# Attention slots of a hybrid encoder layer: VectorE's order of two minima, two normalisations and a gated product

## The chip, the core and the metric

The kernel runs on one core of a Trainium2 chip. Its time is the device time of one execution in microseconds (us), as the median of several runs. A profile of one execution gives, for every engine, the start and duration of each instruction. The engines are TensorE (PE, with its weight loads as PEld), VectorE (DVE), ScalarE (ACT), GpSimd (POOL) and SyncE (SP). Each works through its own instructions in the order in which the program issues them, and they wait for one another through semaphores.

## The reference, cut to what matters

One layer of an encoder on 2048 tokens of width 1024: an adaptive RMSNorm, one input projection, a group of eight neighbourhood-attention heads (head width 64) on a grid of 32 rows by 64 columns, a group of four bidirectional mLSTM heads, an output projection, a residual sum and a last RMSNorm. The change touches the attention:

```python
s = jnp.einsum('bhrcd,bhrjkd->bhrcjk', qg, kg).astype(jnp.float32) + bias[None]
s = jnp.where(col_mask[:, None, :], s, -jnp.inf)
p = jax.nn.softmax(s.reshape(B, NA_HEADS, rows, GRID_W, kh * GRID_W), axis=-1).reshape(s.shape)
o = jnp.einsum('bhrcjk,bhrjkd->bhrcd', p, vg)
...
na_out = neighbourhood_attention(na_q, na_k, na_v, rpb) * jax.nn.silu(na_z)
```

Every query sees a window of 8 rows by 16 columns of keys. The scores get a learned bias, go through a softmax, weigh the values, and the result is multiplied by a gate.

## The kernel before, in words

The input projection and the mLSTM fill the first 1011 us or so of the trace. Then comes the attention stage (`phase2`), in which the output projection runs as filling between the pieces of attention.

**Tiles.** The grid is cut into 16 patches of 8 rows by 16 columns, 128 queries each. A patch sees 11 to 15 rows by 24 or 32 columns of keys, so 264, 288, 352, 360, 384 or 480 scores per query. A *unit* is one patch and one pair of heads (two heads, numbered j = 0 and 1); there are 64 units. A *slot* works on two new units and finishes the two old ones of the slot before: `slot(m)` for m = 0 to 32, of which the last has no new units. The order of all instructions in the stage is the order of the calls (`manual_schedule`); nothing is reordered.

**What a slot issues, by engine, before the change:**

- TensorE: twelve score products into pS (L1341, four buffers, one per unit and head); the old units' value products into pO (L1384, one buffer); six products of the filling (`pump`, L1429: output projection; L866, the last of the input projection, in the first slots); the transposes of the first unit's head 0 (L1369) into pT, which has **one buffer**; five of filling; the transposes of head 1; five; those of the second unit's head 0; four; head 1; four. Slots 0 to 2 have 8, 7, 7, 7, 7 of filling instead.
- VectorE: for each unit and head in turn one pass (L1349) that adds a bias table to the scores, with their sign turned, writes the result into one of four buffers pbuf and returns the row minimum (four *minima* in a slot); then the *normalisation* of the first unit, a reciprocal of its two sums (L1359) and two scalings of pbuf (L1361); then the *gated product* of the old units (L1391), which reads pO; then the normalisation of the second unit.
- ScalarE: behind each minimum the exponential (L1350), in place, with the sum of the row read out from an accumulator; later, behind each group of transposes, the copy of pT into SBUF (L1371). Between them come, where the filling asks for them, squares of finished output rows (L1436; the calls of `finish`), the split of the mixed features into high and low parts (L1399 on ScalarE, L1404 on VectorE), and in the first slots DMA issues and splits of weights.
- SyncE: where the bias table that a minimum has just read isn't needed any more, the load of the table that takes its place (`load_tab`, L1313), issued behind that minimum and used in the next slot; and the queries for two slots later (`load_q`, L1256). GpSimd loads values (L1269), gates (L1279) and rows of x.

In the last filling of a slot VectorE often still adds a finished piece of the output projection to x (L1434), whose square ScalarE issues in the next slot, behind that slot's four exponentials and ahead of its first copy.

**Where it stands in the code.** `scores` (L1327) issues the score products of both units, then minimum, exponential and table load for each unit and head. `normalised` (L1356) issues a unit's reciprocal and scalings, `turned` (L1364) its transposes and copies, `values` (L1374) the value products, `gated` (L1387) the gated product. `slot` (L1545) calls them.

Of the kernel before, what the change touches and what calls it, by code (L numbers as in the profile page):

```python
# [62 lines left out]
class Kernel:  # L63
# [1142 lines left out]
    def phase2(self):  # L1206
# [45 lines left out]
        def load_q(i):  # L1252
            if 2 * i >= NU:
                return
            b, c0 = units[2 * i][0], min(units[2 * i][1], units[2 * i + 1][1])
            (nc.gpsimd, nc.gpsimd, nc.scalar, nc.sync)[min(i, 3)].dma_start(qs[i % 3].bitcast(F32), self.d_qna[:, c0 // 2, b].rearrange("e p c q -> p e c q"))  # L1256
# [53 lines left out]
        def load_tab(u, j):  # L1310
            b, ct = units[u]
            nk = geo[b][4]
            (nc.gpsimd if u < 2 else nc.sync).dma_start(tabs[place[u]][j][:, :nk], self.d_t[PR_T[b // 4]][PC_T[b % 4]][2 * ct + j])  # L1313
# [10 lines left out]
        split, done = set(), []  # L1324
        U = {}

        def scores(pair):  # L1327
            made = {}
            for u in pair:
                b, ct = units[u]  # L1330
                pr, pc, nr, nkc, nk, rpc, nch = geo[b]
                q, c = qs[(u // 2) % 3], ct % 2
                rs = slice(PR_R0[pr], PR_R0[pr] + nr)
                cs = slice(PC_C0[pc], PC_C0[pc] + nkc)
                keys = [kk[ct][:, e * T : (e + 1) * T].rearrange("p (r c) -> p r c", c=GRID_W)[:, rs, cs] for e in range(2)]
                made[u] = [pS.tile([P, 512], F32, tag="pS", name=f"pS_{u}_{j}")[:, :nk] for j in range(2)]
                for n, (e, f) in enumerate(((0, 0), (1, 0), (0, 1))):
                    for j, ps in enumerate(made[u]):
                        js = slice(j * HD, (j + 1) * HD)
                        o = ps.rearrange("p (r c) -> p r c", c=nkc)  # L1340
                        nc.tensor.matmul(o, q[js, e, c, :], keys[f][js], start=(n == 0), stop=(n == 2))  # L1341
            for u in pair:
                nk = geo[units[u][0]][4]
                pts = []
                sums = few.tile([P, 2], F32, tag="sums", bufs=3, name=f"sums_{u}")
                for j, ps in enumerate(made[u]):
                    pt = pbuf[(2 * u + j) % 4]
                    mn = few.tile([P, 1], F32, tag="mn", bufs=4, name=f"mn_{u}_{j}")
                    nc.vector.tensor_tensor_reduce(pt[:, :nk], ps, tabs[place[u]][j][:, :nk], 1.0, 3e38, ALU.add, ALU.min, mn)  # L1349
                    nc.scalar.activation(pt[:, :nk], pt[:, :nk], AF.Exp, bias=mn, scale=-1.0, accum_out=sums[:, j : j + 1])  # L1350
                    pts.append(pt)
                    if u in follows:
                        load_tab(follows[u], j)
                U[u] = (pts, sums)

        def normalised(u):  # L1356
            nk = geo[units[u][0]][4]
            pts, sums = U[u]
            nc.vector.reciprocal(sums, sums)  # L1359
            for j in range(2):  # L1360
                nc.vector.tensor_scalar(pts[j][:, :nk], pts[j][:, :nk], sums[:, j : j + 1], None, ALU.mult)  # L1361
            U[u] = pts

        def turned(u, j):  # L1364
            pr, pc, nr, nkc, nk, rpc, nch = geo[units[u][0]]
            cs = rpc * nkc
            ps = pT.tile([P, 4, P], F32, tag="pT", name=f"pT_{u}_{j}")
            for i in range(nch):
                nc.tensor.transpose(ps[:cs, i, :], U[u][j][:, i * cs : (i + 1) * cs], self.ident)  # L1369
            t = p.tile([P, 4, P], F32, tag="pt", bufs=4, name=f"pt_{u}_{j}")  # L1370
            nc.scalar.activation(t[:cs, :nch, :], ps[:cs, :nch, :], AF.Copy)  # L1371
            U[u][j] = t

        def values(pair):  # L1374
            po = pO.tile([P, 2, P], F32, tag="pO", name=f"pO_{pair[0]}")
            for u in pair:
                b, ct = units[u]
                nch = geo[b][6]
                pt = U.pop(u)
                for i in range(nch):  # L1380
                    v, n = L[b]["v"][i]
                    for j in range(2):
                        h = 2 * ct + j
                        nc.tensor.matmul(po[j * HD : (j + 1) * HD, ct % 2, :], v[:n, h * HD : (h + 1) * HD], pt[j][:n, i, :], start=(i == 0), stop=(i == nch - 1))  # L1384
            return po

        def gated(pair, po):  # L1387
            b, ct = units[pair[0]]
            c0 = ct // 2 * 2
            z = zs[pos[b] % 2][:, c0 : c0 + 2, :]  # L1390
            nc.vector.tensor_mul(z, po, z)  # L1391
# [120 lines left out]
        def loads(n):  # L1512
            b, ct = units[n]
            i = n % 4
            nb = after.get(b)
            if b == last_b and i == 1:
                load_x(b)
            if nb is not None and i:
                load_v(nb, 1 if i < 3 else 4)
                if i == 2 and b != b0:  # L1520
                    load_z(nb)
# [8 lines left out]
        def step():  # L1530
            if self.between:
                self.between.pop(0)()
            self.step_todo()

        def finish():
            while self.squares:
                self.squares.pop(0)()

        def mixed(b, half):
            mix_high(b, half)  # L1540
            mix_low(b, half)
            if half:
                self.queue.append(outproj(b))

        def slot(m):  # L1545
            new = (2 * m, 2 * m + 1) if 2 * m < NU else ()
            old = (2 * m - 2, 2 * m - 1) if m else ()
            if m:
                load_q(m + 2)
            if new:  # L1550
                scores(new)
            if old:
                po = values(old)
            if new:
                normalised(new[0])
            if old:
                gated(old, po)
            if new:
                normalised(new[1])
            b = units[old[0]][0] if m > 2 and old[0] % 4 == 2 else None  # L1560
            if not new:
                mixed(b, 1)
                mixed(b, 0)
                for _ in range(2):
                    self.pump(12)
                    finish()
                    step()
                return
            fills = [8, 7, 7, 7, 7] if m < 3 else [6, 5, 5, 4, 4]
            for n in range(-1, 4):  # L1570
                if n >= 0:
                    turned(new[n // 2], n % 2)
                    if n % 2:
                        step()
                    finish()
                    if n in (1, 2) and b is not None:
                        mixed(b, n % 2)
                    if n in (0, 2):
                        loads(new[n // 2])
                    if n == 1 and self.reloads:  # L1580
                        self.reloads.pop(0)()
                for fn in extra.pop((m, n), ()):
                    fn()
                self.pump(fills[n + 1])
            if m == 2:
                self.pump(max(0, self.left) + 1)
                self.owed = 0
                mixed(b0, 1)
                mixed(b0, 0)

        with self.tc.manual_schedule():
            for m in range(NU // 2 + 1):
                slot(m)
            while len(done) < len(patches):
                finish()
                while self.between:
                    self.between.pop(0)()
                while self.todo:
                    self.todo.pop(0)()
                self.pump(24)  # L1600
            for fn in self.between + self.todo:
                fn()
# [77 lines left out]
```

## Time and profile before

| what | value |
|---|---|
| runs | 1382.79, 1383.26 and 1388.96 us; median 1383.26 |
| profiled execution | 1385.16 us |
| its span, first to last instruction | 1383.4 us |
| mean granted clock of TensorE | 0.989 |
| slots of the attention stage | 32 with new units, beginning at 1015.2 to 1344.9 us of the span |
| length of a slot | 9.4 to 12.8 us |

The span is the time from the first to the last instruction of the profiled execution; 1.8 us of the execution lie around it. In a row of a timeline stand the start in us from the span's beginning, the duration, the engine, the line, the operation and its operands (out<-in), and in square brackets how long the engine had been idle before it and what released it. Rows of groups give the busy time in us, the mean in ns, and the idle time ahead with its releasers. Consecutive instructions of one engine overlap in such rows by about a tenth of a microsecond, since they are pipelined.

### The profile page before, as it was taken

What the parts mean: (1) busy time and instruction counts of PE and PEld (TensorE: products, weight loads), DVE (VectorE), ACT (ScalarE), POOL (GpSimd) and SP (SyncE); (2) the same over time, 40 slices, a digit from 0 to 9 for tenths busy, and PEclk for the clock granted to TensorE, in tenths of its full rate; (3) what the DMA queues carried; (4) which work ended last, traced back from release to release, by engine and by line L of the source; (5) the groups of instructions that cost most, each with busy time, mean ns of one, the idle gap of its engine ahead of it and who ended that gap; (6) DMA issues with size and microseconds to landing.
All of it is one profiled execution on the core that took longest, in us unless ns stands there. A gap on an engine that the chain in (4) does not pass through costs nothing.

```text
span 1383.4 us, 23357 instructions
## 1 busy us (share of the span) xinstructions
PE 1291.3 (93%) x8204; PEld 1104.9 (80%) x8204; DVE 792.3 (57%) x2428; ACT 531.8 (38%) x1123; POOL 284.1 (21%) x306
## 2 busy tenths in 40 slices
PE   2989998998999999999989999899998999999996
PEld 2889998998887778788878878778876777778775
DVE  6683324111355569246767866767736666667664
ACT  4642334423232233213313322323346555555552
POOL 4343212424101011001212101212201211112121
PEclk9999999999999999999999999999999999999998
DMA  9799449787557685554675788555588996867871
GB/s 321 223 290 228 122 97 238 175 204 189 149 110 210 151 191 160 164 157 144 184 219 182 229 237 284 165 159 159 176 249 251 209 228 171 187 184 183 205 182 47
DMA packets 243272, 263.29 MB, mean 190 GB/s; under 512 B 31814, under 2 KB 200006, under 8 KB 243154
## 3 DMA queue, kind: packets, MB, share of 16 engines
q1 hardware_dynamic: 151774, 186.18, 49.8%
q0 software_dynamic: 20496, 36.21, 10.8%
q10 hardware_dynamic: 70884, 39.40, 9.9%
q8 instruction: 65, 1.06, 0.3%
q14 instruction: 53, 0.43, 0.1%
HBM read 177.18 MB, written 92.72 MB: 195 GB/s over the span
## 4 chain that ended last, share of the span: by engine, by line
PE 46%; DMA 11%; issue 4%; DVE 4%; POOL 1%; ACT 1%; ACTq 0%; SPq 0%; DVEq 0%; POOLq 0%
PE pq L866 19%; PE y L1429 9%; DMA tab<-d_t 4%; PE pT L1369 3%; PE pO L1384 2%; PE pS L1341 2%; PE pi L1090 2%; DMA kv<-d_ck 2%; PE px L1088 2%; PE pc L429 2%; PE pc L430 2%; PE pc L431 2%; DMA d_mix<-zt 2%; PE dc L1036 1%; DMA d_qna<-qst 1%
## 5 line engine op out<-in xcount | busy, mean ns | idle before, releaser
L866 PE MATMUL pq<-hhi,whi_a 128*128 128x512 f32 x512 | 208.6, 407 | 1.2 <-ACT u L773 0.8
L866 PE MATMUL pq<-hlo,whi_a 128*128 128x512 f32 x512 | 208.9, 408 | 0.0
L866 PE MATMUL pq<-hhi,wlo_a 128*128 128x512 f32 x512 | 208.2, 407 | 0.0
L866 PEld LDWEIGHTS pq<-hhi,whi_a 128*128 128x128 f32 x512 | 97.3, 190 | 18.9 <-ACT u L773 1.2
L866 PEld LDWEIGHTS pq<-hlo,whi_a 128*128 128x128 f32 x512 | 97.2, 190 | 16.8 <-issue 0.5
L866 PEld LDWEIGHTS pq<-hhi,wlo_a 128*128 128x128 f32 x512 | 97.3, 190 | 16.6
L1371 ACT ACTIVATE pt<-pT 96x384 f32<-96x384 f32 (+3 forms) x128 | 65.8, 514 | 84.5 <-PE pT L1369 81.3
L1350 ACT ACTIVATE pbuf<-pbuf,mn 128x480 f32<-128x480 f32 (+5 forms) x128 | 76.1, 595 | 54.1 <-DVE mn L1349 53.8
L1429 PE MATMUL y<-hhi,whi_a 128*128 128x512 f32 x256 | 90.6, 415 | 0.5 <-ACT whi_a L1399 0.5
L1429 PE MATMUL y<-hhi,wlo_a 128*128 128x512 f32 (+1 forms) x272 | 90.6, 399 | 0.2 <-ACT y L1436 0.2
L1349 DVE CUSTOM_DVE_ANT_0 pbuf<-pS,tab 128x480 f32<-128x480 f32 (+5 forms) x128 | 63.3, 540 | 40.3 <-PE pS L1341 29.6
L840 POOL TENSOR_TENSOR wlo_a<-rawq,whi_a 128x1024 fp32r<-128x1024 f32 x20 | 48.6, 2430 | 169.8 <-ACT whi_a L839 144.9
L1112 POOL TENSOR_TENSOR hm<-hm,ck 128x128 f32<-128x128 f32 x64 | 26.4, 413 | 260.3 <-DVE hm L1111 183.4
L429 PE MATMUL pvo<-whi_b,hhi 128*128 128x256 f32 x256 | 74.1, 289 | 5.7 <-DVE stvo L499 5.7
L1093 ACT ACTIVATE num<-px,gtile 128x129 f32<-128x129 f32 x120 | 38.3, 366 | 105.7 <-PE px L1088 88.0
L1020 DVE TENSOR_SCALAR wv<-kv,gtile 128x129 f32<-128x129 f32 x120 | 38.4, 329 | 67.1 <-DMA kv<-d_ck 33.5
L1369 PE MATMUL pT<-ident,pbuf 128*128 128x128 f32 (+2 forms) x416 | 66.8, 273 | 10.0 <-DVE pbuf L1361 8.5
L1369 PEld LDWEIGHTS pT<-ident,pbuf 128*128 128x128 f32 (+2 forms) x416 | 50.3, 136 | 31.9 <-issue 11.6
L430 PE MATMUL pvo<-wlo_b,hhi 128*128 128x256 f32 x256 | 72.8, 285 | 0.0
L431 PE MATMUL pvo<-whi_b,hlo 128*128 128x256 f32 x256 | 72.8, 284 | 0.0
L714 ACT ACTIVATE dec<-dec,gtile 128x128 f32<-128x128 f32 x128 | 42.0, 392 | 71.4 <-POOL dec L710 68.3
L499 DVE TENSOR_TENSOR stvo<-pvo,brow 128x256 f32<-128x256 f32 x64 | 26.5, 419 | 68.6 <-PE pvo L431 56.4
(295 smaller groups left out, 3432.6 us busy)
## 6 DMA issues: line engine op xcount, KB each, us to landing
ck<-d_ck SPq DMA_DIRECT2D x64, 384.5 KB
kv<-d_ck SPq DMA_DIRECT2D x120, 128.5 KB
rawq<-in_w_main_dram SPq DMA_DIRECT2D x28, 512.0 KB
raw<-in_w_main_dram SPq DMA_DIRECT2D x20, 512.0 KB
d_ck<-stvo SPq DMA_DIRECT2D x16, 514.0 KB
x<-in_x_dram SPq DMA_DIRECT2D x16, 512.0 KB
wada<-in_w_ada_dram SPq DMA_DIRECT2D x32, 256.0 KB
dec<-d_mneg SPq DMA_DIRECT2D x32, 256.0 KB
```

What stands on the lines that cost most here:

```text
L429: nc.tensor.matmul(ps, lhi(k), rhi(k), start=(k == 0), stop=False)
L430: nc.tensor.matmul(ps, lhi(k), rlo(k), start=False, stop=False)
L431: nc.tensor.matmul(ps, llo(k), rhi(k), start=False, stop=(k == KT - 1))
L714: nc.scalar.activation(t[:, d, o, :], t[:, d, o, :], AF.Exp, bias=self.cols["g"][:, d, h, c : c + 1])
L840: nc.gpsimd.tensor_tensor(lo[:, :, cs], raw, hi[:, :, cs].bitcast(F32), ALU.subtract)
L866: nc.tensor.matmul(patch_ps(ps) if patch else ps, w, self.htok(h, g, k, patch), start=(k == 0 and n == 0), stop=(k == KT - 1 and n == 2))
L1020: nc.vector.tensor_scalar(wv, tiles[d, i][:, 128:257], self.cols["w"][:, d, h, c : c + 1], None, ALU.mult)
L1349: nc.vector.tensor_tensor_reduce(pt[:, :nk], ps, tabs[place[u]][j][:, :nk], 1.0, 3e38, ALU.add, ALU.min, mn)
L1350: nc.scalar.activation(pt[:, :nk], pt[:, :nk], AF.Exp, bias=mn, scale=-1.0, accum_out=sums[:, j : j + 1])
L1369: nc.tensor.transpose(ps[:cs, i, :], U[u][j][:, i * cs : (i + 1) * cs], self.ident)
L1371: nc.scalar.activation(t[:cs, :nch, :], ps[:cs, :nch, :], AF.Copy)
L1429: nc.tensor.matmul(y, m[:, k, :], w[k][:, cs], start=(k == 4 and n == 0), stop=(k == 3 and n == 2))
```

## The change

`scores` is cut in two. `products` issues the score products of both units, `scored` the minima, the exponentials and the table loads. Between the first unit's and the second unit's minima `scored` now calls `normalised` for the first unit. The gated product follows when `scored` is done, so behind the second unit's minima; the second unit's normalisation stays last. On TensorE, ScalarE, SyncE and GpSimd the order of instructions stays the same; on VectorE it becomes: two minima, normalisation of the first unit, two minima, gated product, normalisation of the second unit.

```diff
-        def scores(pair):
+        def products(pair):
             made = {}
             for u in pair:
...
                         nc.tensor.matmul(o, q[js, e, c, :], keys[f][js], start=(n == 0), stop=(n == 2))
+            return made
+
+        def scored(pair, made):
             for u in pair:
                 nk = geo[units[u][0]][4]
...
                 U[u] = (pts, sums)
+                if u == pair[0]:
+                    normalised(u)
...
             if new:
-                scores(new)
+                scored(new, products(new))
             if old:
-                po = values(old)
-            if new:
-                normalised(new[0])
-            if old:
-                gated(old, po)
+                gated(old, values(old))
             if new:
                 normalised(new[1])
```

## The prediction

> **What bounds the kernel now.** I began with the page: its first table says which engine has no room.
>
> ```profile
> PE 1291.3 (93%) x8204; PEld 1104.9 (80%) x8204; DVE 792.3 (57%) x2428; ACT 531.8 (38%) x1123; POOL 284.1 (21%) x306
> ```
>
> TensorE works 93% of the span and VectorE 57%, so a VectorE order can matter only where TensorE waits for it. The change touches the attention stage alone (1011 to 1355 us of the trace), so next comes the table of waits of TensorE and VectorE in that window (engine and line, released by: total us, times, longest):
>
> ```profile
> PE pT L1369 <- DVE pbuf L1361: 8.5, 6, 2.2
> PE pT L1369 <- ACT pt L1371: 1.6, 1, 1.6
> ...
> DVE pbuf L1349 <- DMA tab<-d_t: 9.8, 11, 2.5
> ```
>
> Six times in 32 slots a slot's first transposes wait for the normalisation, 8.5 us in all. That is the most that the change can win. Everywhere else TensorE runs through, and the question is whether it still will.
>
> Third I read the timeline of one slot engine by engine: slot 29, an ordinary one of 360 scores (start, duration, engine, line). VectorE:
>
> ```profile
> 1326.77 0.53 DVE L1349 CUSTOM_DVE_ANT_0 pbuf<-pS,tab 128x360 f32<-128x360 f32 x1
> ...
> 1328.64 0.17 DVE L1359 RECIPROCAL sums<-sums 128x2 f32<-128x2 f32 x1
> 1328.84 0.73 DVE L1361 TENSOR_SCALAR pbuf<-pbuf,sums 128x360 f32<-128x360 f32 x2
> 1329.48 0.42 DVE L1391 TENSOR_TENSOR zs<-pO,zs 128x256 f32<-128x256 f32 x1
> ```
>
> ScalarE and TensorE in the same slot:
>
> ```profile
> 1327.93 0.58 ACT L1350 ACTIVATE pbuf<-pbuf,mn 128x360 f32<-128x360 f32 x1
> 1328.42 0.18 ACT L1350 ACTIVATION_READ_ACCUMULATOR pbuf<-pbuf,mn 128x1 f32 x1
> 1328.51 0.58 ACT L1350 ACTIVATE pbuf<-pbuf,mn 128x360 f32<-128x360 f32 x1
> ...
> 1329.09 0.58 ACT L1350 ACTIVATE pbuf<-pbuf,mn 128x360 f32<-128x360 f32 x1
> ...
> 1329.67 0.58 ACT L1436 ACTIVATE y<-xr 128x512 f32<-128x512 f32 x1
> ...
> 1330.28 0.47 ACT L1371 ACTIVATE pt<-pT 120x384 f32<-120x384 f32 x1
> ```
> ```profile
> 1329.53 0.49 PE L1369 MATMUL pT<-ident,pbuf 128*120 128x128 f32 x3
> ...
> 1331.03 0.49 PE L1369 MATMUL pT<-ident,pbuf 128*120 128x128 f32 x3
> ```
>
> See the coupling. pT has one buffer. The second transposes (1331.03) may start only when the copy of the first (L1371) has left pT, and on ScalarE that copy stands behind all four exponentials and, here, a square (L1436). It ends at 1330.28 + 0.47 = 1330.75, 0.28 us before TensorE arrives. So the exponentials of the second unit lie on TensorE's path already, with almost nothing to spare.
>
> **What the change moves.** No instruction is added or removed. On VectorE the minima of the second unit go behind the first unit's reciprocal and its two scalings. The reciprocal needs both exponentials of the first unit, so VectorE now stands still for them with the second minima queued behind. Today that wait is covered: by the time four minima are done the exponentials are too (reciprocal 1328.64, accumulator read out by 1328.42 + 0.18 = 1328.60). Slot 0 shows the naked hand-overs:
>
> ```profile
> 1018.41 0.19 ACT L1350 ACTIVATION_READ_ACCUMULATOR pbuf<-pbuf,mn 128x1 f32 x1
> ...
> 1021.41 0.49 ACT L1371 ACTIVATE pt<-pT 96x384 f32<-96x384 f32 x1 [2.81 <-DMA v<-d_vna]
> ```
> ```profile
> 1018.63 0.17 DVE L1359 RECIPROCAL sums<-sums 128x2 f32<-128x2 f32 x1 [0.19 <-ACT pbuf L1350]
> ```
> ```profile
> 1021.95 0.53 PE L1369 MATMUL pT<-ident,pbuf 128*96 128x128 f32 x3 [1.57 <-ACT pt L1371]
> ```
>
> ScalarE to VectorE: 1018.63 - 1018.60 = 0.03. Copy's end to transposes: 1021.95 - 1021.90 = 0.05.
>
> *Shift of the second exponentials, slot 29.* Readout ends 1328.60; + 0.03 reciprocal; + 0.20 to the scalings (1328.64 to 1328.84); + 0.73 for both; - 0.09, by which the next instruction overlaps them (1329.48 against 1329.57); + 0.53 minimum; + 0.04 to its exponential: 1330.04 instead of 1328.51, a shift of **1.53 us**. In general it is 0.27 + pair of scalings + one minimum. Other widths come from VectorE's groups by form (busy, mean ns of one):
>
> ```profile
> L1349 DVE CUSTOM_DVE_ANT_0 pbuf<-pS,tab 128x480 f32<-128x480 f32 x32 | 19.4, 653 | 9.6 <-PE pS L1341 9.0 <-DMA tab<-d_t 0.6
> ...
> L1361 DVE TENSOR_SCALAR pbuf<-pbuf,sums 128x480 f32<-128x480 f32 x32 | 14.0, 479 | 0.6
> ...
> L1349 DVE CUSTOM_DVE_ANT_0 pbuf<-pS,tab 128x264 f32<-128x264 f32 x16 | 6.3, 430 | 6.6 <-DMA tab<-d_t 4.2 <-PE pS L1341 1.7 <-PE pO L1384 0.7
> ...
> L1361 DVE TENSOR_SCALAR pbuf<-pbuf,sums 128x264 f32<-128x264 f32 x16 | 5.1, 362 | 0.3
> ```
>
> A pair overlaps by 0.10 (2 x 0.415 against 0.73). 480 wide: 0.27 + 0.86 + 0.65 = 1.78. 264 wide: 0.27 + 0.62 + 0.43 = 1.32.
>
> *Slots with a square before the copy.* Slot 29: copy at 1330.28 + 1.53 = 1331.81, done 1332.28, transposes 1332.33 instead of 1331.03: **+1.30**. Slot 11 (480 wide) and slot 31 (288 wide):
>
> ```profile
> 1141.61 0.58 ACT L1436 ACTIVATE y<-xr 128x512 f32<-128x512 f32 x1
> ...
> 1142.63 0.60 ACT L1371 ACTIVATE pt<-pT 128x512 f32<-128x512 f32 x1 [0.31 <-PE pT L1369]
> ```
> ```profile
> 1143.54 0.60 PE L1369 MATMUL pT<-ident,pbuf 128*128 128x128 f32 x4
> ```
> ```profile
> 1348.63 0.58 ACT L1436 ACTIVATE y<-xr 128x512 f32<-128x512 f32 x1
> ```
> ```profile
> 1350.34 0.49 PE L1369 MATMUL pT<-ident,pbuf 128*96 128x128 f32 x3
> ```
>
> A copy can follow a square 0.61 after its start (1329.67 to 1330.28). Slot 11: 1142.22 + 1.78 + 0.60 + 0.05 = 1144.65, **+1.11**. Slot 31: 1349.24 + 1.32 + 0.49 + 0.05 = 1351.10, **+0.76**. Such slots are the odd ones from 5 on except 17, 25, 27, which wait for tables: four of 352 to 384 scores (9, 15, 23, 29), four of 480 (11, 13, 19, 21), three near slot 31 (5, 7, 31): 5.2 + 4.4 + 2.3 = 11.9.
>
> *Slots without a square.* Slot 28:
>
> ```profile
> 1318.85 0.58 ACT L1350 ACTIVATE pbuf<-pbuf,mn 128x360 f32<-128x360 f32 x1
> ```
> ```profile
> 1321.34 0.49 PE L1369 MATMUL pT<-ident,pbuf 128*120 128x128 f32 x3
> ```
>
> Without a square the copy could start at the last exponential's end, 1318.85 + 0.58 = 1319.43. With the shift: 1319.43 + 1.53 + 0.49 (the copy, as in slot 0) + 0.05 = 1321.50: +0.16. The narrow ones fit with no wait, the widest pass it somewhat; I take 0.2 for twelve even slots (bounds 0 and 0.7): 2.4.
>
> *The six that wait today.* Slot 17, the longest:
>
> ```profile
> 1204.64 0.56 DVE L1349 CUSTOM_DVE_ANT_0 pbuf<-pS,tab 128x384 f32<-128x384 f32 x1 [2.30 <-DMA tab<-d_t]
> ```
> ```profile
> 1207.13 0.47 ACT L1371 ACTIVATE pt<-pT 128x384 f32<-128x384 f32 x1
> ```
> ```profile
> 1206.48 0.52 PE L1369 MATMUL pT<-ident,pbuf 128*128 128x128 f32 x3 [2.21 <-DVE pbuf L1361]
> ...
> 1208.00 0.49 PE L1369 MATMUL pT<-ident,pbuf 128*128 128x128 f32 x3
> ```
>
> The late table belongs to the second unit, so the first transposes lose their 2.21 us of waiting. But the second ones still need the copy behind that table's exponentials: 1207.13 + 0.47 + 0.05 = 1207.65 instead of 1208.00. Of 2.21 us only 0.35 stays won: a wait on VectorE ahead of the first transposes turns into one on ScalarE ahead of the second. Slot 8 has no square:
>
> ```profile
> 1110.99 0.52 PE L1369 MATMUL pT<-ident,pbuf 128*128 128x128 f32 x3 [1.02 <-DVE pbuf L1361]
> ```
>
> Its 1.02 us I count as won whole. In slots 3 and 4 all four minima start late, so the first transposes go on waiting, and the second wait as in any slot with some room: +0.85 each. Slot 27, once free of its table, is nearly an ordinary squared slot, +0.6; slot 25, narrow, comes out even. Together -0.35 - 1.0 + 1.7 + 0.6 = +1.0 (bounds: -8.5, all won, and 6 x 1.1 = 6.6, a squared slot's price on each).
>
> *Slot 0* waits for the copy already (1.57), with ScalarE's load issues behind the exponentials: the full shift, +1.3. Slots 1 and 2 have more filling and lose nothing.
>
> TensorE, the bound, has nothing of its own to catch up with, so every pause is paid in full.
>
> **Sum: 11.9 + 2.4 + 1.0 + 1.3 = +16.6 us.** The profiled execution took 1385.16 us (span 1383.40), which becomes 1401.8; the median of the runs, 1383.26, becomes **1400**.
>
> What else moves costs nothing, and here is its cover. The gated product goes 0.9 later (behind the last minimum); its next reader across engines, the split of the mix or the next values into pO, comes later by more. In slot 29 the second unit's scalings start behind its exponentials (1329.67 + 1.53 = 1331.20 and 0.2 to 0.3 of hand-over) and end near 1332.2; its transposes, one more step of 1.50 (1329.53 to 1331.03) behind the second ones, come at 1333.8. SyncE reloads each table behind the minimum that read it, so the second unit's tables are issued 1.3 to 1.8 us later; their use in the next slot moves as far, and the queue is full:
>
> ```profile
> 1191.49 3.76 SPq L1313 DMA_DIRECT2D tab<-d_t  x4
> ```
>
> Four issues held for 3.76 us, and the last table's minimum starts only at 1204.64: these loads wait for the transfers ahead.
>
> **Rivals.**
> *Faster: only the first transposes matter.* If the second exponentials still got out before TensorE needed pT, the six waits would go: 1383.3 - 8.5 = 1375. It decides where the room before the second transposes exceeds the shift of 1.3 to 1.8. The room is the transposes' start less the earliest end of the copy and 0.05: 0.23 (slot 29), 0.67 (slot 11), 1.37 (slot 28); only the narrow slots without a square pass. The Trainium skill, Perfetto Trace Analysis, Optimization Strategy, says to find what blocks the gaps of the limiting engine and make those dependencies start sooner; by that rule alone this rival would win. 4%.
> *Half.* Something I take as serial overlaps (scalings shorter, squares later): +8, 1391. 12%.
> *Late tables too.* If in slots 8, 17, 25, 27 the tables did land 1.9 later, 4 x 1.9 = 7.6 more: 1408. Against it speaks the full queue. 9%.
> *The clock drops.* Many new pauses of TensorE could lower its clock. Windows of the trace (after the window: PE, PEld, DVE, ACT, POOL busy; then granted clock, DMA share, GB/s):
>
> ```profile
> 862.00:867.50 5.50, 2.12 (x9) 1.46 (x9) 0.00 (x0) 0.69 (x2) 0.00 (x0) 1.00 0.52 199
> 867.50:874.30 6.80, 4.05 (x13) 3.37 (x14) 6.03 (x17) 3.73 (x9) 2.75 (x2) 0.50 0.72 194
> ...
> 1203.00:1207.00 4.00, 1.79 (x10) 1.25 (x9) 2.30 (x9) 1.80 (x7) 0.00 (x0) 1.00 1.07 243
> ```
>
> A pause in the first window is followed by 6.8 us at half clock, 3.4 us lost; eleven such would give 1400 + 37 = 1437. But 2.21 us of waiting at 1204 left 1.00, and the new pauses are below 1.5. The Trainium skill, TensorE: Matmul & The Clock Gate, HAM oscillation, puts the rule at idle gaps over about 3.4 us, and the section on psum-queue depth-cycling lets frequent short ones do it too; the rows fit the first. 2%.
> *No effect*, all inside covers I misread: 1383. 3%.
>
> **Numbers.** The forecast has 70%, within 1394 to 1406 (0.2 us either way in some 30 slots). Half a per cent, 6.9 us, is about what a measurement of this kernel can tell from no change. Slower by more: 0.70 + 0.12 + 0.09 + 0.02 = 0.93; within: 0.03; faster: 0.04. From the half case to the late tables, with their own spread: 1389 to 1411.
>
> **What would show it.** TensorE's waits in the stage should show the transposes waiting for ScalarE's copy some 20 times, about 20 us, and hardly for VectorE. In slot 29 the second minima should start 1.5 us after the first pair's end, and the squared slots should be 0.8 to 1.3 us longer. The waits of the minima on tables (9.8 us, 11 times) should shrink, since the second minima come later than the tables. If the copy does not start later, if the pauses still stand before the first transposes, or if tables land later than now, a step is wrong.

## The result, and the profile after

The changed kernel takes 1402.56 us (median of six runs, 1399.82 to 1410.08) against 1383.03 us (six runs, 1381.01 to 1388.96): a ratio of 1.0145, 95% interval 1.0113 to 1.0176. It is slower, by 1.1 to 1.8%. The forecast was 1400 us. The profiled execution took 1402.41 us, its span 1400.6 us, at a mean granted clock of 0.987 (0.989 before).

In the lines of the changed kernel the minima stand at L1352, the exponentials at L1353, reciprocal and scalings at L1364 and L1366, the transposes at L1374, their copies at L1376, the gated product at L1396, the output projection at L1434, the addition to x at L1439 and the square at L1441. The page's first table, of after:

```profile
PE 1298.5 (93%) x8204; PEld 1106.8 (79%) x8204; DVE 797.4 (57%) x2428; ACT 530.8 (38%) x1123; POOL 285.0 (20%) x306
```

The instructions are the same in number. TensorE's busy time is 7 us more, and its share of 93% looks like the one of before: this table doesn't show what went wrong. The waits of the attention stage do (after; engine and line, released by: total us, times, longest):

```profile
PE pT L1374 <- ACT pt L1376: 22.9, 25, 3.5
PE pT L1374 <- DVE pbuf L1366: 3.5, 2, 1.9
```
```profile
DVE sums L1364 <- ACT pbuf L1353: 47.9, 64, 1.0
...
DVE pbuf L1352 <- DMA tab<-d_t: 0.8, 3, 0.3
```

Before, the transposes waited 8.5 us for VectorE and 1.6 us for ScalarE. Now it is 3.5 and 22.9: four of the six waits that the new order could take away are gone, and 24 others have come, at another place. On VectorE every one of the 64 reciprocals now waits for its exponentials, 47.9 us in all, and the waits of the minima for their tables have shrunk from 9.8 us to 0.8.

Slot 29 shows one of the new waits. VectorE, ScalarE and TensorE of after (start, duration, engine, line):

```profile
1342.24 0.53 DVE L1352 CUSTOM_DVE_ANT_0 pbuf<-pS,tab 128x360 f32<-128x360 f32 x1
...
1343.65 0.17 DVE L1364 RECIPROCAL sums<-sums 128x2 f32<-128x2 f32 x1 [0.88 <-ACT pbuf L1353]
1343.85 0.73 DVE L1366 TENSOR_SCALAR pbuf<-pbuf,sums 128x360 f32<-128x360 f32 x2
1344.49 0.53 DVE L1352 CUSTOM_DVE_ANT_0 pbuf<-pS,tab 128x360 f32<-128x360 f32 x1
```
```profile
1345.12 0.60 ACT L1353 ACTIVATE pbuf<-pbuf,mn 128x360 f32<-128x360 f32 x1 [1.50 <-DVE mn L1352]
...
1345.71 0.58 ACT L1353 ACTIVATE pbuf<-pbuf,mn 128x360 f32<-128x360 f32 x1
...
1346.29 0.58 ACT L1441 ACTIVATE y<-xr 128x512 f32<-128x512 f32 x1
...
1346.91 0.47 ACT L1376 ACTIVATE pt<-pT 120x384 f32<-120x384 f32 x1
```
```profile
1340.43 0.76 PE L1341 MATMUL pS<-hlo,qs 64*128 64x360 f32 x6
...
1345.82 0.39 PE L1434 MATMUL y<-hlo,wlo_a 128*128 128x512 f32 x1
1347.43 0.54 PE L1374 MATMUL pT<-ident,pbuf 128*120 128x128 f32 x3 [1.22 <-ACT pt L1376]
```

Read it as a chain: VectorE stands still for 0.88 us and then normalises the first unit, so the second unit's minima come later, so ScalarE stands still for 1.50 us in front of their exponentials, the square and the copy follow, and TensorE stands still for 1.22 us in front of its second transposes. The slot begins at 1340.43, so these stand at +7.00 in it. Before the change they stood at 1331.03 - 1325.41 = +5.62, the slot's start being taken from the trace. It is 1.38 us longer.

Slot by slot (start to start, by the score products' rows of both traces, in the groups of the prediction):

| slots | predicted | measured |
|---|---|---|
| eleven with a square ahead of the copy | +11.9 | +13.8 |
| twelve even ones without a square | +2.4 | +4.0 |
| six that waited for VectorE (17: -0.92, 8: -0.82, 3: +1.11, 4: +0.76, 27: +0.60, 25: +0.22) | +1.0 | +0.9 |
| slot 0 | +1.3 | +3.5 |
| sum | +16.6 | +22.2 |

The squared slots 9, 15, 23 and 29 are 1.39, 1.58, 1.39 and 1.38 us longer, the four with 480 scores 1.22 or 1.23 each. (Slot 31 is counted here by what follows slot 30; from slot 0 to the start of slot 31 the time went from 329.7 to 351.0 us, +21.3. That stretch is called *the stage* below.) The profiled execution of after got to slot 0 5.0 us earlier than that of before, in work that the change doesn't touch; in the twelve traces of this study that start lies between 1004.5 and 1015.2 us. So the span grew by 17.2 and not by 22.2. Times of runs carry this scatter; the stage doesn't, and the experiments are read by both. Each experiment was timed beside the kernel before in a series of its own; the median of the kernel before lay between 1371.66 and 1383.03 us in them, so ratios and stages can be compared from one experiment to the next, and times in us can't.

How do the waits add up to the +22.2? The waits of the transposes went from 8.5 + 1.6 to 22.9 + 3.5 us, slot 31 included, which is 16.3 us more. Two things more are needed, and both are in the rows. A pause costs more than its idle time: products of the filling start 0.23 us apart and overlap in the rows, so that without the wait the transposes of slot 29 would have started at 1345.82 + 0.23 = 1346.05. They came 1.38 later, of which only 1.22 is idle: 0.16 more. In most other slots with a single pause it is 0.20 to 0.25 us (slot 11: 1.22 longer, 1.02 idle; slot 18: 1.22 and 0.98). There are 20 more pauses than before, which at 0.2 us each makes an estimate of 4.0 us. And slot 0 is longer by about 1.5 us more than its longer wait (3.5 less 1.96), which the section on the clock explains. 16.3 + 4.0 + 1.5 = 21.8 of 22.2.

### The profile page after: what moved, and what is told of

The parts are those of the page before. It is cut to its first block, busy times and chain, and to the rows that moved or that the text cites. A ratio compares the mean times of both kernels' runs of the same rounds, so it can differ in the third digit from the quotient of the medians.

```text
span 1400.6 us, 23355 instructions
## 1 busy us (share of the span) xinstructions
PE 1298.5 (93%) x8204; PEld 1106.8 (79%) x8204; DVE 797.4 (57%) x2428; ACT 530.8 (38%) x1123; POOL 285.0 (20%) x306
## 4 chain that ended last, share of the span: by engine, by line
PE 36%; DMA 8%; issue 7%; ACT 7%; DVE 6%; POOL 1%; SPq 0%; ACTq 0%; POOLq 0%; DVEq 0%
PE pq L866 16%; PE y L1434 6%; ACT pbuf L1353 4%; DMA kv<-d_ck 2%; DMA tab<-d_t 2%; PE pT L1374 2%; PE pi L1090 2%; DVE pbuf L1352 2%; PE pc L429 2%; PE pc L431 2%; PE pc L430 2%; PE px L1088 1%; PE pS L1341 1%; PE dc L1036 1%; DMA hlo<-d_wo 1%
## 5 line engine op out<-in xcount | busy, mean ns | idle before, releaser
L1353 ACT ACTIVATE pbuf<-pbuf,mn 128x480 f32<-128x480 f32 (+5 forms) x128 | 76.4, 598 | 98.0 <-DVE mn L1352 98.0
L1374 PE MATMUL pT<-ident,pbuf 128*128 128x128 f32 (+2 forms) x416 | 68.3, 277 | 26.4 <-ACT pt L1376 22.9
L1374 PEld LDWEIGHTS pT<-ident,pbuf 128*128 128x128 f32 (+2 forms) x416 | 49.0, 136 | 54.3 <-ACT pt L1376 38.1
L1434 PE MATMUL y<-hhi,whi_a 128*128 128x512 f32 x256 | 90.7, 416 | 0.7 <-ACT whi_a L1404 0.7
L1434 PE MATMUL y<-hhi,wlo_a 128*128 128x512 f32 (+1 forms) x272 | 90.5, 399 | 0.2 <-ACT y L1441 0.2
L1376 ACT ACTIVATE pt<-pT 96x384 f32<-96x384 f32 (+3 forms) x128 | 65.2, 509 | 63.3 <-PE pT L1374 59.5
L1352 DVE CUSTOM_DVE_ANT_0 pbuf<-pS,tab 128x480 f32<-128x480 f32 (+5 forms) x128 | 64.4, 537 | 28.4 <-PE pS L1341 27.5
```

Source lines behind the costliest of these rows:

```text
L1434: nc.tensor.matmul(y, m[:, k, :], w[k][:, cs], start=(k == 4 and n == 0), stop=(k == 3 and n == 2))
```

## The experiments

The theory, as predicted: the second unit's exponentials were on TensorE's path already, through the copy that stands behind them on ScalarE and through pT's one buffer. Against it stood that VectorE's own standing still is the price, wherever the copy stands (theory two), that the table loads come later and hold the next slots (theory three), that the second unit's normalisation comes late for the third transposes, and the clock.

### Undoing only the coupling

**The square early.** One line is added to the changed kernel: the square of the filling is issued behind the first unit's two exponentials, ahead of the second unit's.

```diff
                 if u == pair[0]:
                     normalised(u)
+                    finish()
```

> The changed kernel with the waiting squares issued on ScalarE between the first and the second unit's exponentials, where ScalarE stands idle for 1.5 us. Nothing changes on VectorE. Theory (TensorE pauses because the copy out of pT stands on ScalarE behind the second unit's later exponentials and the square): 11 slots with a square lose 0.61 us less each, 6.7 us in all, so about 1396 against 1402.6, and the second transposes' waits on the copy fall from 22.9 to about 16 us. Rival one (VectorE's own stand of 47.9 us for the first exponentials is what costs): no change, 1402 to 1403. Rival two (the second unit's normalisation is late for the third transposes): no change.

Measured: ratio 1.0108 (1.0072 to 1.0144), 1394.32 us against 1379.69; stage 341.7. Waits of the transposes, with all lines one further down:

```profile
PE pT L1375 <- ACT pt L1377: 13.6, 23, 3.0
PE pT L1375 <- DVE pbuf L1367: 2.1, 2, 1.9
```

Moving the squares on ScalarE, with VectorE's order unchanged, takes 9.3 of the 21.3 us away. It was to be 6.7, for eleven squares. The line moves fourteen: the slots 17, 25 and 27 have one too and became 0.5 to 0.6 us shorter each, 1.6 together. The ten squared slots of the stage (5 to 29) gave 6.4 us, 0.6 in most, as expected; the rest is mostly slots 0 and 4 (0.5 and 1.4 shorter) against slot 6 (0.55 longer). In slot 29 the pause is down to 0.59 us, and what is left ahead of the copy are the exponentials alone.

**The first copy between the exponentials.** On top of that, the very last exponential of a slot is issued behind the first copy, and the second unit's normalisation behind that exponential. VectorE's order in front of the second minima stays as in the changed kernel.

```diff
-                    nc.scalar.activation(pt[:, :nk], ..., AF.Exp, ...)
+                    if u != pair[0] and j:
+                        last.append(exp)
+                    else:
+                        exp()
...
+                    if n == 0:
+                        last.pop(0)()
+                        normalised(new[1])
```

> The changed kernel with the squares early as in the first run and, on ScalarE, the first copy out of pT ahead of the last exponential instead of behind it; the second unit's normalisation on VectorE follows that exponential. VectorE keeps standing still for the first unit's exponentials. Theory: the pauses at the second transposes go nearly all, what is left is slot 0 (some 3 us), slots 3 and 4 (some 4 us) and a few tenths at the third transposes of the narrower squared slots: 1385, between 1380 and 1389. If the early normalisation is worth anything, this is near or below the kernel before. Rival one (VectorE's stand costs): still above 1398. Rival two (normalisation of the second unit late): slower than 1402, since that normalisation is later still.

Measured: ratio 1.002 (0.9995 to 1.0046), 1382.44 us against 1379.69; stage 329.6, that of before. Waits of TensorE and of VectorE in the stage:

```profile
PE pT L1381 <- ACT pt L1383: 4.0, 6, 3.0
PE pT L1381 <- DVE pbuf L1373: 3.0, 4, 1.9
```
```profile
DVE sums L1371 <- ACT pbuf L1355: 66.3, 64, 4.6
```

VectorE now stands 66.3 us in front of its reciprocals, more than in the changed kernel, and the stage is no longer than before. So the standing of VectorE is not the price (theory two falls); what ScalarE has to do ahead of the copy is. The second unit's normalisation is later still in this kernel, and all four waits for a normalisation that are left stand at a slot's first transposes (slots 3, 4, 7, 8), none at the second unit's; so its lateness isn't the price either. Two moves on ScalarE, with that normalisation following one of them, give the net 21.3 us back. It is a balance: slots 8, 17, 25 and 27 are 4.1 us shorter together than before the change, slot 4 is 1.1 shorter, and slots 0, 3, 7, 9, 15 and 18 are 4.7 us longer. ScalarE and TensorE in slot 29 of this kernel: the copy ends at 1326.65 + 0.47 = 1327.12, ahead of the last exponential, and the transposes start 0.05 later, after 0.03 us of idle time in the trace:

```profile
1326.56 0.19 ACT L1355 ACTIVATION_READ_ACCUMULATOR pbuf<-pbuf,mn 128x1 f32 x1
1326.65 0.47 ACT L1383 ACTIVATE pt<-pT 120x384 f32<-120x384 f32 x1
1327.02 0.58 ACT L1355 ACTIVATE pbuf<-pbuf,mn 128x360 f32<-128x360 f32 x1
```
```profile
1327.17 0.54 PE L1381 MATMUL pT<-ident,pbuf 128*120 128x128 f32 x3
```

### Are the tables part of it?

Both kernels without the reloads of the bias tables, the change alone between them:

```diff
-                    if u in follows:
-                        load_tab(follows[u], j)
```

> The kernel before without the reloads of the bias tables: the first four tables stay (behind zeros), so the scores of later units get a wrong bias. Theory: four of the six waits at the first transposes (slots 8, 17, 25, 27: 1.02 + 2.21 + 0.92 + 0.60 = 4.8 us) come from late tables and go, those of slots 3 and 4 stay at 1.9 and 1.8 us: 1378. Rival: the waits at the first transposes are VectorE's own lateness and stay: 1383.

> The changed kernel without the reloads of the bias tables, as in the run of the kernel before without them. Theory: the tables are hardly waited for any more in the changed kernel (0.8 us on VectorE), so taking them away wins at most 1.5 us: 1401 to 1403, and against the kernel before without tables the change costs 23 to 24 us instead of 19.5. Rival (later table loads are a part of the loss): 5 us faster or more, below 1398.

Measured: 0.9961 (0.9943 to 0.998) for the old order, 1.0164 (1.0125 to 1.0203) for the new one; stages 323.4 and 347.3. With no table to wait for, the change costs 23.9 us of stage, not less than the 21.3 with them. One forecast missed: the changed kernel was to win at most 1.5 us by this and won 3.7 (351.0 to 347.3), still short of the rival's 5. Of these, 2.0 lie in slot 0 (14.28 us instead of 16.25), where the clock did not drop this time (below). The transposes of the old order and of the new one, in this pair:

```profile
PE pT L1367 <- DVE pbuf L1359: 4.0, 3, 1.9
PE pT L1367 <- ACT pt L1369: 0.9, 1, 0.9
```
```profile
PE pT L1372 <- ACT pt L1374: 21.7, 24, 3.0
PE pT L1372 <- DVE pbuf L1364: 3.1, 2, 1.9
```

The waits for ScalarE are there all the same, so theory three falls. The old order's four waits behind late tables are gone, as expected (4.0 us in 3 waits are left of 8.5 in 6). The pair also prices the tables in the old order: 329.7 - 323.4 = 6.3 us of stage.

### How much of VectorE's order is needed

**One minimum ahead.** The first unit's normalisation is put behind the second unit's first minimum, half-way to the old order.

```diff
+                    if u != pair[0] and j == 0:
+                        normalised(pair[0])
...
-                if u == pair[0]:
-                    normalised(u)
```

> A half step: VectorE normalises the first unit behind the second unit's first minimum, so that only one minimum is moved. VectorE still waits for the first exponentials, for half as long. Theory: only the second unit's last exponential is later, by about 1.0 us in slots of 360 and 1.2 in those of 480, less the room ahead of the second transposes: squared slots lose 0.8, 0.5 and 0.4 us (352 to 384, 480, narrow) instead of 1.4, 1.2 and 1.0, slots without a square nothing, and slots 8 and 17 still win their 0.8 to 0.9. Stage 337 to 340 us (329.7 before, 351.0 changed), time +8 us against the kernel before, ratio 1.006. Rival (any stand of VectorE in this place costs by itself): half of the loss in every slot, those without a square included, +10 us.

Measured: ratio 1.0054 (1.0029 to 1.008), stage 337.4, 9.0 us of waits for the copy. About half the shift costs about a third of the price (7.7 of 21.3 us, of which slot 0, where the clock dropped again, has 2.5), since what is shorter than the room is hidden: the slots without a square are back at their old lengths (12: 11.01, 28: 9.68). One point was wrong. Slot 17 was to win 0.8 to 0.9 us and stayed at 12.04 (12.21 before): there the second unit's first minimum is the one that waits for its table, 1.49 us in this run, and it still stands ahead of the normalisation.

**Only where it wins.** The old order in 28 slots; in the four slots whose second tables come late (8, 17, 25, 27) the new order, with the square early and the copy between the exponentials.

> The old order in 28 slots, and in the four slots that wait for late tables (8, 17, 25, 27) the early normalisation together with the copy ahead of the last exponential and the square early. Theory: these four win what they won in the run with the copy between (2.1 + 1.1 + 0.5 and up to 0.4 us), the others stay as before: stage 325.5 to 326.5 us against 329.7, time 3 to 4 us under the kernel before, ratio 0.997 to 0.998. Rival (the early normalisation wins nothing by itself): ratio 1.000, stage 329 to 330.

Measured: ratio 0.9995 (0.997 to 1.002). The four slots are shorter, as expected (8: 9.95, 17: 10.08, 25: 9.43, 27: 9.93; they were 10.93, 12.21, 10.56 and 10.51). Not all of it is kept: in slot 9, behind slot 8, the second unit's first minimum waits 0.80 us for its table, and the slot takes 10.38 us instead of 9.72. And the stage is 327.2 instead of 325.5 to 326.5; slot 4 took 13.51 us instead of 11.71, since the clock had dropped there (below). A gain of 2.5 us of stage can't be told from no change in the times of the runs.

### Is it the one buffer?

**Two banks.** The second head's transposes go into the bank of the value products, which is free by then, so that TensorE's second transposes need not wait for the first copy. The change, and the old order, with it:

```diff
-            ps = pT.tile([P, 4, P], F32, tag="pT", ...)
+            ps = (pO if j else pT).tile([P, 4, P], F32, tag="pO" if j else "pT", ...)
```

> The changed kernel, every engine's order untouched, with the transposes of a unit's second head put into the bank of pO (free by then: the gated product has read it) instead of pT. Theory (the loss runs over pT's single buffer): the second transposes no longer wait for the first copy, the pauses of 22.9 us go, and what the early normalisation wins in slots 8, 17, 25 and 27 stays; the waits at the first transposes of slots 3 and 4 remain (3.5 us). Stage 324 to 327 us against 329.7 before and 351.0 changed, slot 0 back near 12.8, ratio to the kernel before 0.995 to 0.999. Rivals (VectorE's stand for the exponentials, a late normalisation of the second unit): the stage stays above 340.

> The kernel before with the same second bank. Theory: only the 1.6 us of slot 0 is won, the six waits for the normalisation (8.5 us) stay: stage 327.5 to 329 us, ratio 0.998 to 1.000; the run of the changed kernel with the second bank is then 3 to 4 us shorter than this one in the stage, which is what the early normalisation is worth with nothing behind it. Rival (the second bank helps by itself): 325 or less.

Measured: the changed kernel 1.0041 (1.0023 to 1.0058), stage 332.8; the old order 1.0012 (0.999 to 1.0033), stage 329.9. The buffer is the link: 18.2 of the 21.3 us are gone without touching the order of anything, and between these two kernels the change costs 2.9 us (332.8 less 329.9) where it cost 21.3. Both stages missed what was expected. The old order was to take 327.5 to 329: six waits for the normalisation stayed, as foretold (8.3 us). But of the 1.8 us that slot 0 won slot 1 lost 1.2, waiting for its values, and slot 17 took 14.27 us instead of 12.21, with a stretch at half clock in it, so that the difference to the changed kernel understates the change by about 2 us. The changed kernel should have come to 324 to 327. Tables are a part of the reason: slot 25 took 11.08 us (10.56 before), its first unit's second minimum having waited 1.50 us for its table, and slot 27 took 11.19 (10.51). A new row shows the larger part (waits of the changed kernel with two banks):

```profile
PE pT L1374 <- DVE pbuf L1366: 5.2, 6, 1.8
PE y L1434 <- ACT y L1441: 2.8, 10, 0.4
PE pT L1374 <- ACT pt L1376: 1.0, 1, 1.0
```

The square writes its squares into y, the PSUM tile of the filling (the program uses its sum alone). Products of the next piece need that tile, and the square stands behind the late exponentials just as the copy does. Slot 15 of that kernel:

```profile
1176.84 0.58 ACT L1441 ACTIVATE y<-xr 128x512 f32<-128x512 f32 x1
```
```profile
1176.70 0.48 PE L1434 MATMUL y<-hhi,whi_a 128*128 128x512 f32 x1
1177.60 0.50 PE L1434 MATMUL y<-hhi,whi_a 128*128 128x512 f32 x1 [0.42 <-ACT y L1441]
```

Slot 15 is 11.36 us long there, like in the changed kernel, and 1.57 longer than before. The square has less than half of that: the slot's first transposes had already waited 0.51 us for the normalisation, with 0.48 us of waiting for a table ahead of it, and the lag is 0.86 us before the product of 1177.60 and 1.55 behind it. In slot 29, 0.7 of its 0.96 us come with the square. That was a reading after the fact, so it was put to a test.

**Two banks and the square early.** The line of the first experiment on top of the two banks.

> The changed kernel with the second head's transposes in the bank of the value products, and with the square issued right behind the first unit's exponentials. With two banks alone the stage took 332.8 us, 18.2 of 21.3 us of the change's cost gone, and the slots 9, 11, 13, 15, 19, 21, 23 and 29 stayed 0.2 to 1.6 us longer than before the change. Theory: there the square is the holder; it writes into the PSUM tile that the next product of the filling needs, and stands behind the late second exponentials. Issued early it lets the tile go, and these eight slots come within 0.3 us of their old lengths (slot 15 to 10.1 or less, slot 29 to 10.0 or less): stage 327.5 to 329.5, ratio 0.998 to 1.002. Slots 3, 4, 25 and 27, whose first transposes wait for VectorE, stay as they were. Rival: the tile isn't what holds them, but something else that comes late with the second exponentials, such as the split of the mix or the second unit's transposes: stage 332 to 333.5, slot 15 at 11.2 or more, ratio 1.003 to 1.005.

Measured: stage 327.3, ratio 0.9967 (0.9944 to 0.999), 1372.77 us against 1378.91. Slot 15 is 9.78 us long (9.79 before the change), slot 29 9.70 (9.74); 11, 13, 19 and 21 are at 10.95 to 10.99, 23 at 9.72. TensorE's waits for the square are down from ten to one (0.2 us), and one wait for the copy is left, in slot 0:

```profile
PE pT L1375 <- DVE pbuf L1367: 4.4, 4, 1.8
PE pT L1375 <- ACT pt L1377: 1.2, 1, 1.2
...
PE pT L1375 <- DVE zs L1397: 0.4, 1, 0.4
```

Slot 29's copy starts in it at +5.88, a whole microsecond later than before the change, and its second transposes at +5.62, where they were. The lateness is still there; nothing that TensorE needs stands behind it any more. Of the eight slots named one missed: slot 9 is 10.67 us long (9.72), its first unit's second minimum having waited 1.08 us for its table and the first transposes 0.69 us behind it. Slots 3, 25 and 27 did not stay as they were either. 25 came down from 11.08 to 9.46, as its table was waited for 0.23 us instead of 1.50; 27 came to 10.83, with 1.30 us of waiting for a table; 3 went from 12.59 to 13.02, where a product of the filling waits 0.91 us instead of 0.48 for a split of weights on ScalarE. So of the 5.5 us between the two kernels with two banks some 3.9 lie in the eight slots named, of which slot 15's 0.9 ahead of its square are the table's. Waits for the square had stood in slots 7, 17, 25 and 27 too; what of the rest is the square's and what the tables', these two runs don't separate. The last row shown is a price of the second bank: in slot 5 the second transposes wait for the gated product, which has to read that bank first. This version beats the kernel before by the interval, by a little: 0.1 to 0.6%. In the stage 2.4 us are won, 0.17% of the time; where the interval reaches further, the stage doesn't explain it.

### The clock in slot 0

Slot 0 was mis-sized by 2.2 us. Windows of after (us; PE, PEld, DVE, ACT, POOL busy; granted clock, DMA share, GB/s):

```profile
1016.27:1019.69 3.42, 0.79 (x5) 0.75 (x6) 0.23 (x1) 1.28 (x3) 0.00 (x0) 1.00 0.60 177
1019.69:1023.10 3.41, 3.41 (x11) 2.62 (x11) 1.75 (x2) 1.64 (x3) 0.00 (x0) 0.50 0.87 269
```

A pause is followed by 3.4 us at half clock. That the pause is the cause was tried by giving slot 0 alone its old order:

```diff
-                if u == pair[0]:
+                if u == pair[0] and u:
                     normalised(u)
```

> The changed kernel with slot 0 alone in the old order. Theory: slot 0 grew from 12.75 to 16.25 us because ScalarE's load issues, and the first copy behind them, follow the second unit's exponentials (1.5 to 2.0 us), and because the pause of 3.5 us was followed by a stretch at half clock (about 1.5 us). With the old order slot 0 is back at 12.6 to 12.8 us with no stretch at half clock in it, slots 1 to 31 stay as in the changed kernel, and the stage from slot 0's to slot 31's start goes from 351.0 to 347.5 us. Rival (slot 0 is long for reasons outside of the order, such as loads): it stays above 15.

Measured: slot 0 takes 12.51 us at a granted clock of 1.00 throughout; the stage 346.7, 4.3 us less than after. Of these, 3.7 lie in slot 0; slot 4 is 1.4 shorter too, and slot 5 is 0.4 longer. The one time taken is 1397.75 us, beside a median of 1375.88 for the kernel before, whose own runs lie up to 12 us apart there: one run can't show 4 us either way.

## Why the prediction was right

**The chain held step by step.** The second exponentials of slot 29 were to start 1.53 us later. They started at 1345.12, +4.69 in the slot, against 1328.51 - 1325.41 = +3.10: 1.59. The copy followed behind them and the square, and the second transposes behind the copy. The 1.30 became 1.38, by hand-overs a little longer than those taken (an exponential started 0.10 us after its minimum's end, where 0.04 was taken). Summed over eleven squared slots that is 13.8 for 11.9: the right mechanism, 0.1 us short in most (0.3 in slots 7 and 15, 0.5 in slot 5). One sign of the prediction was misworded: 1.5 us is the shift of the exponentials. The minima move by the same terms without one minimum and its hand-over, to 1328.60 + 0.03 + 0.20 + 0.73 - 0.09 = 1329.47 instead of 1327.67, which is 1.80, and they did (+4.06 in the slot against +2.26).

**The six waits** gave the net of +0.9 that was worked out (+1.0). Slot 17 won 0.92 instead of 0.35, slot 8 won 0.82 instead of 1.0. In slot 17 the table that held the second unit's minimum until +4.77 before the change was no longer waited for at +4.15 after it, so the late table that the prediction counted on was gone, and its second transposes waited 1.29 us for the copy like those of a squared slot. So a wait in front of the first transposes did turn into one in front of the second; that the sum came out so close is partly luck, since single slots are off by up to 0.6 us. Rival one, the gain of 8.5 us, falls: of all that waiting only 1.7 us came back.

**The even slots** were to cost 0.2 each and cost 0.33 on average, between -0.1 and 1.2, where the bounds had been 0 to 0.7. The widest pay: the slots of 480 scores (10, 12, 18, 20) 0.4 to 1.2. Of the others only 16, 26 and 28 pay, 0.4 to 0.5.

**Slot 0 is the step that was off**: 3.5 for 1.3. The shift of its second transposes was 1.94 instead of 1.3 (between the last exponential and the copy, where ScalarE issues loads, 0.54 us more went by than in the profile of before), and then came the half clock. The rival "the clock drops" came true at one place only, for 1.5 us or so.

**What hid the rest hid it.** The tables were to land no later, and the pair without reloads shows that they are not the price; the waits on tables shrank to 0.8 us, as said. Some 20 waits for the copy of 20 us in all were foretold, and there are 25 of 22.9 us. The gated product, 0.9 later, delayed nothing that any view shows.

**The sum** was 16.6 and the stage with slot 31 gave 22.2: 1.9 of the difference lie in the squared slots, 1.6 in the even ones, 2.2 in slot 0. The forecast came within 3 us of the median all the same, since the medians differ by 19.5: runs vary by some microseconds in the work ahead of the stage, so that the closeness is partly luck.

## What to carry to other kernels

When an instruction is moved ahead on one engine, look for what now stands behind it in that engine's queue, and follow that to the bound engine: here two minima came 1.8 us later in slot 29, and on the next engine the copy that frees the only buffer, and on which the third one waits, came 1.6 us later. The room at that far point, the start of the waiting instruction less the earliest end of what it needs (0.23 us here, against a shift of 1.5), decides; the sum of waits in front of the moved instruction (8.5 us) says only what could be won at most. And when a link is cut, look for the second holder: an output that nobody reads still occupies the bank that it is written to.

## What the runs showed of the hardware that was not expected

**Less than a whole idle window lowers the clock.** The prediction held pauses below 2.2 us to be harmless, and took the rows to fit a limit of about 3.4 us of idle time. Two kernels had nearly the same pause in slot 0, 3.00 us with the square early and 2.95 us with the copy between the exponentials. The first, cut at the edges of the half-clock stretch:

```profile
1012.96:1016.37 3.41, 1.03 (x6) 0.94 (x7) 0.47 (x1) 1.52 (x3) 0.00 (x0) 1.00 0.69 179
1016.37:1019.79 3.42, 3.42 (x11) 2.62 (x10) 1.50 (x2) 1.57 (x3) 0.00 (x0) 0.50 0.91 280
```

The second, cut on the same grid of 3.413 us as its own half-clock stretches elsewhere begin on:

```profile
1014.40:1017.81 3.41, 2.17 (x11) 1.50 (x10) 0.99 (x5) 0.63 (x2) 0.00 (x0) 1.00 0.49 123
1017.81:1021.22 3.41, 1.69 (x9) 1.48 (x10) 1.16 (x4) 1.95 (x5) 0.00 (x0) 1.00 0.75 240
1021.22:1024.64 3.42, 3.42 (x19) 2.65 (x19) 1.54 (x2) 1.92 (x3) 0.00 (x0) 1.00 0.87 263
```

In the first most of the pause (2.4 us) falls into one window, of which TensorE is busy 1.03 / 3.41 = 30%; the next runs at half clock. In the second it is split between two windows, busy 64% and 50%, and the clock stays. The changed kernel without table reloads had a pause of 3.01 us there, split between windows of 49% and 62%, and the clock stayed too: its slot 0 took 14.28 us, that of the kernel with the square early 15.75. In every trace the half-clock stretches begin at whole multiples of 3.413 us from one another. A shorter pause can do it too, where other gaps fall into the same window. In the kernel with the new order only in the late slots, slot 4 (its longest single wait there was 2.0 us):

```profile
1062.73:1066.14 3.41, 1.38 (x9) 0.89 (x8) 3.38 (x13) 2.42 (x8) 0.39 (x1) 1.00 0.52 158
1066.14:1069.56 3.42, 3.42 (x11) 2.71 (x11) 0.94 (x4) 0.97 (x3) 2.10 (x4) 0.50 0.86 205
```

Busy 40%, and half clock next. With one minimum ahead, a window of 46% was followed by full clock:

```profile
1054.27:1057.68 3.41, 1.57 (x8) 1.14 (x8) 2.50 (x11) 2.55 (x9) 0.81 (x2) 1.00 1.01 281
1057.68:1061.10 3.42, 3.32 (x20) 2.72 (x20) 2.91 (x4) 3.42 (x6) 0.00 (x0) 1.00 1.07 340
```

In the windows of the stage, over all these traces, those of 22 to 40% busy were followed by half clock and those of 46% and more were not. The rest of the traces narrows it and limits it. From 60 us on, every window at full clock that was less than 45% busy was followed by half clock and none over 46% was. In the first 50 us that doesn't hold: in ten of the twelve traces a window of 46 to 65% there was followed by half clock, and windows in which TensorE did nothing were not. So the busy share of one window isn't the whole rule; it is a reading of the traces that no run puts to a test. The Trainium skill, TensorE: Matmul & The Clock Gate, What's actually happening, describes a free-running window of 3413 ns; the grid here agrees with that. Its figure of one idle window as the condition does not hold here as it stands: none of the windows shown was idle throughout, and 40% busy did not keep the clock up. So a pause of 2 to 3.5 us costs up to 1.7 us more (half a window) or not, by where it falls, and a version that shortens such a pause can win or lose that by chance.
